# Rows 1024 to 2047 of w_down in pairs by seven products, in both layers of a hybrid attention trunk

## The chip, the cores and the metric

One NeuronCore of one Trainium2 chip runs the whole kernel in one launch. The metric is the time of one execution on the device, in microseconds, median of several runs. The kernel before takes 1486.2 us (1485.95 to 1486.5 in three runs).

## What is computed

Two layers over 512 tokens of width 1024, float32. Each has two attention mixers, and then the part that is at issue here, a squared-ReLU MLP with a residual:

```python
h = rmsnorm(x, norm_mlp)
return x + jnp.square(jax.nn.relu(h @ w_up)) @ w_down
```

w_up is 1024 x 4096, w_down 4096 x 1024. After the second layer comes a last rmsnorm. Products are computed to float32 accuracy from two parts each: every operand is split into a rounded part (hi) and what remains (lo), and TensorE takes hi x hi, hi x lo and lo x hi, three matmuls for one.

## The kernel before, in words

Activations stand transposed, with 128 features on the partitions and the 512 tokens along the free dimension. x is eight tiles of 128 x 512.

**Plain products** are blocks of 128 x 128 weights against 512 columns (`gemm`, L244 to L246, three matmuls a block). Their weights come by SP's DMA queue in pieces of 128 x 1024 (`fetch`, L202), in an order written out by hand (`order`); `convert` makes hi on ScalarE (L218) and lo on VectorE (L219), one piece ahead of the use.

**Seven products** (a Strassen scheme in Winograd's form) take the place of eight for a 2 x 2 block product: 256 of the rows, 256 of the contraction's halves and 256 tokens. `Strassen.unit` computes one of 16 units of w_up, 256 hidden features each: products a11, s1, a12, s2, a22, s3, s4, each of twelve matmuls of 256 columns (`narrow`, L1535). s2 and s3 add onto a11's bank, s4 onto s1's. The sums of the left operand are made from two raw blocks: r2 and r1 are loaded by SP, POOL's queue adds one half of r2 to the other while transferring (L1487), a third block is loaded and added to as well (L1495, L1496), and `convert` of Strassen adds (L1522, L1525) and splits into hi and lo (L1515, L1516). A unit runs the conversion of the next unit between its products. ScalarE and VectorE take the results out of PSUM into z (L1557 to L1577), `act` applies relu, the norm's factor and the square (L1598, L1599), and splits the result into hi and lo (L1600, L1601). The list `acts` gets two entries a unit, so entries 4c to 4c+3 are the rows 512c to 512c+511 of w_down.

**w_down**: rows 0 to 3071 go plainly, in six chunks of four blocks of rows. For each chunk and each of the eight column blocks m, one plain result of twelve 512-column matmuls (`down` in `mlp`) is added to x[m] by VectorE (L1124). `DOWNS` says how many of these 48 results follow each unit; three are left over for after unit 15:

```python
DOWNS = 0, 0, 3, 4, 3, 4, 4, 4, 4, 4, 4, 3, 3, 2, 2, 1
```

Rows 3072 to 4095 go by seven products: `combine`, called for units 12 to 15, forms the sums of the right operand from z (L1292 to L1299), and `Strassen.down` (S.down in the text) computes four pairs of column blocks behind it (L1323) and adds them to x (L1342 to L1364). Its first products are a11 and a12 of two tiles, then s2 and so on; a11 takes the even act entries, a12 the odd ones, s2 the sums. It is followed by the next layer, or by the output.

`load(g)` is issued two units ahead. Every engine's queue runs in order, SP's and POOL's included; the order within a queue is set at build time and need not be the order of the code. Tiles are shared by tags with a number of buffers each (`BUFS`), and a new use waits for the last reader of the old.

Of the kernel before, what the change touches and what calls it, by code (L numbers as in the profile page):

```python
# [18 lines left out]
D = 1024  # L19
T = 512  # L20
# [65 lines left out]
def layout(a):  # L86
# [3 lines left out]
    for l in range(L):  # L90
# [53 lines left out]
class Body:  # L144
# [8 lines left out]
    BUFS = dict(raw=2, wh=2, wl=2, u2=8, o2=8, va=4, t2=12, kd=2, kk=1, zz=4, zzm=2, pt=10, long=2, q2=3, q2m=1, vn=1, e=2, cp=2, a4=4, b4=4, f=2, h=2, tmp=3,  # L153
# [42 lines left out]
    def fetch(self):  # L196

        if self.plan and self.plan[0] is not None:
            src, n, *tag = self.plan.popleft()
            tag = tag[0] if tag else self.raws.popleft() if self.raws else "raw"  # L200
            raw = self.t(tag, [128, 1024], name="raw")
            self.nc.sync.dma_start(raw[:, :n], src)  # L202
            self.loaded.append((raw, src, n))
# [419 lines left out]
    def compress(self, kc, vc, small, l):  # L623
# [3 lines left out]
        for x, pos in ((kc, "pos_k"), (vc, "pos_v")):  # L627
            t = [self.t("t2", [128, 8, 2, 32], name="ca") for _ in range(2)]
            v = x.rearrange("p (n j r) -> p r j n", j=8, r=2)
            for half in range(2):  # L630
                nc.vector.memset(t[half][:, :, 1, 31], 0.0)
# [138 lines left out]
    def setup(self, first):  # L770
# [15 lines left out]
        self.kcz = t[:, 512:1280].rearrange("p (h f n) -> p h f n", h=2, f=2)  # L786
        self.vz = t[:, 1408:1920].rearrange("p (h r d) -> p h r d", h=2, r=2)
# [50 lines left out]
    def order(self, l):  # L838
# [23 lines left out]
        yield from ((a["wd2"][l, c, m], 1024) for c in range(6) for m in range(4))  # L862

    def layer(self, l, u):
# [227 lines left out]
        for m in range(8):  # L1092
# [20 lines left out]
    DOWNS = 0, 0, 3, 4, 3, 4, 4, 4, 4, 4, 4, 3, 3, 2, 2, 1  # L1113

    def mlp(self, l, x, S, acc):
# [4 lines left out]
        def down(c, m, w):  # L1120

            ps = self.p(self.short())
            yield from self.gemm(ps, w, 4 * (m % 2), acts[4 * c:4 * c + 4], ks=4)
            nc.vector.tensor_add(x[m], x[m], ps)  # L1124

        def downs():
            for c in range(6):
# [56 lines left out]
    def go(self):  # L1184
# [20 lines left out]
        self.xs = [self.dp.tile([128, T], F32, name=f"xs{k}") for k in range(KT)]  # L1205
        self.x_src = [a["xT"][k] for k in range(KT)]
# [10 lines left out]
class Strassen:  # L1217
# [9 lines left out]
    def __init__(self, body, l, x, gm):  # L1227
        self.b, self.nc, self.l, self.x, self.gm = body, body.nc, l, x, gm
        self.raw, self.ops = {}, {}
        self.c, self.t, self.twice, self.made, self.done = [], [], [], 0, set()  # L1230
# [56 lines left out]

    AHEAD = 8

    def combine(self, p):  # L1290

        b, V = self.b, self.nc.vector  # L1292
        v = self.c[p].rearrange("p a c -> p (a c)").rearrange("p (k c) -> p k c", c=256)
# [6 lines left out]
        self.t.append(o)  # L1300

    def down(self, acts):
# [9 lines left out]
        def side(k):  # L1312
            if k not in known:
                i = dict(s1=0, s2=3, s3=1, a22=2)[k]
                known[k] = [(t[:, i, 0], t[:, i, 1]) for t in self.t]
            return known[k]

        def product(k, g, onto=None):
# [6 lines left out]
            if self.twice:  # L1325
                xs, self.twice = xs[:2] + self.twice, []
# [129 lines left out]
    def source(self, g, i):  # L1456
        a = self.b.a
        return (a["wup"][self.l, 2 * g + i] if g < 16 else a["wdn"][self.l, 2 * g + i - 32]).rearrange("p k c -> p (k c)")

    def load(self, g, third=True):  # L1460

        b = self.b
        if g > 17:
            r = b.t("vn", [128, 2, 1024], name="raw") if g == 18 else b.t("kk", [128, 4, 1024], name="raw")[:, :2]
# [3 lines left out]
        else:  # L1468
# [5 lines left out]
            if g < 2:  # L1474
                for t in (r2, r1, s3):
# [167 lines left out]
```

## Time and profile before

| | |
|---|---|
| median of three runs | 1486.2 us |
| profiled execution, first to last instruction | 1485.2 us |
| TensorE matmuls busy | 1477.2 us |
| TensorE weight loads busy | 1290.5 us |
| VectorE busy | 1137.4 us |
| ScalarE busy | 804.7 us |
| GpSimd (POOL) busy | 109.1 us |
| moved by DMA | 203.65 MB |
| granted TensorE clock | 0.997 of 2.4 GHz |

The profiled execution's total time outside its span is not given; the span is 1.0 us below the median of the runs. Busy matmul time is modelled at the ends and overlaps, so distances between starts tell more than durations. PEld is TensorE's weight load, which runs beside the matmuls; DVE is VectorE, ACT ScalarE, SP and POOL the other two engines with DMA queues. In layer 0 the MLP's units run from 412.6 to 688 us, S.down from 699.5 to about 740 us.

### The profile page before, as it was taken

Reading aid. Unit: us, or ns where it says so; the run is one execution under the profiler, and the core shown is the slowest. Engines: PE = TensorE matmul, PEld = TensorE weight load, DVE = VectorE, ACT = ScalarE, POOL = GpSimd, SP = SyncE. Lnnn points to the kernel's source line nnn. Section 1 sums busy time; section 2 is a strip of 40 time slices with the busy share of each in tenths; the row PEclk is TensorE's granted clock in tenths of the full one; section 3 lists DMA queues with packets and bytes.
Section 4 is the critical chain, followed back from the end, with each engine's and each line's share of the span. In section 5 each row is a group of like instructions: output and inputs, shape, how many; then the busy total and the mean of one; then the engine's idle time right before and its main releaser. Section 6 shows DMA issues by size and latency. Waiting matters only on the chain.

```text
span 1485.2 us, 23423 instructions
## 1 busy us (share of the span) xinstructions
PE 1477.2 (99%) x8766; PEld 1290.5 (87%) x8766; DVE 1137.4 (77%) x2247; ACT 804.7 (54%) x1533; POOL 109.1 (7%) x159
## 2 busy tenths in 40 slices
PE   9999999999999999999999999999999999999998
PEld 8887888888899988999988788888888999999998
DVE  5688988777986767779746789787679977667885
ACT  6465655554774444456444656555447644444554
POOL 1010000001000000002010000000010100000121
PEclk9999999999999999999999999999999999999998
DMA  7554522126554555456256543221274645545561
GB/s 272 168 152 128 165 71 72 57 72 206 176 138 127 156 154 142 143 149 184 79 197 181 167 118 114 80 77 58 97 216 128 176 142 148 146 123 147 156 143 57
DMA packets 75649, 203.65 MB, mean 137 GB/s; under 512 B 9456, under 2 KB 10864, under 8 KB 75536
## 3 DMA queue, kind: packets, MB, share of 16 engines
q1 hardware_dynamic: 58832, 172.24, 35.9%
q0 software_dynamic: 12672, 23.07, 9.3%
q10 hardware_dynamic: 4032, 6.84, 1.3%
q8 instruction: 69, 1.13, 0.3%
q14 instruction: 44, 0.36, 0.1%
HBM read 151.72 MB, written 4.19 MB: 105 GB/s over the span
## 4 chain that ended last, share of the span: by engine, by line
PE 95%; DVE 2%; issue 1%; ACT 0%; DMA 0%; POOL 0%; POOLq 0%; SPq 0%; DVEq 0%; ACTq 0%
PE ps_mm L244 12%; PE ps_mm L245 12%; PE ps_mm L246 12%; PE ps_S L1535 9%; PE ps_PT L1535 6%; PE ps_O L244 3%; PE ps_O L245 3%; PE ps_O L246 3%; PE ps_mm L1535 3%; PE ps_O L1535 3%; PE ps_O L614 3%; PE ps_PT L587 2%; PE ps_S L562 2%; PE ps_mm L1323 2%; PE ps_S L1323 2%; PE ps_PT L472 1%
## 5 line engine op out<-in xcount | busy, mean ns | idle before, releaser
L218 ACT CAST wh<-raw 128x1024 fp32r<-128x1024 f32 (+2 forms) x161 | 164.5, 1023 | 147.3 <-PE ps_O L245 81.1
L219 DVE TENSOR_TENSOR wl<-raw,wh 128x1024 fp32r<-128x1024 f32 (+2 forms) x161 | 191.8, 1192 | 17.8 <-ACT wh L218 14.8
L244 PE MATMUL ps_mm<-u,wh 128*128 128x512 f32 x480 | 192.4, 401 | 0.2
L245 PE MATMUL ps_mm<-u,wh 128*128 128x512 f32 x480 | 189.3, 394 | 0.0
L246 PE MATMUL ps_mm<-u,wl 128*128 128x512 f32 x480 | 188.9, 393 | 0.0
L1516 DVE TENSOR_TENSOR s<-raw,s 128x1024 fp32r<-128x1024 f32 (+1 forms) x128 | 138.9, 1087 | 32.5 <-ACT s L1515 31.3
L244 PE MATMUL ps_mm<-o,wh 128*128 128x512 f32 x344 | 134.6, 391 | 0.0
L245 PE MATMUL ps_mm<-o,wh 128*128 128x512 f32 x344 | 134.5, 391 | 0.0
L246 PE MATMUL ps_mm<-o,wl 128*128 128x512 f32 x344 | 134.2, 390 | 0.0
L1515 ACT CAST s<-raw 128x1024 fp32r<-128x1024 f32 (+1 forms) x128 | 118.0, 942 | 20.7 <-PE ps_PT L1535 9.1
L244 PEld LDWEIGHTS ps_mm<-u,wh 128*128 128x128 f32 x480 | 90.3, 188 | 20.0 <-issue 1.5
L246 PEld LDWEIGHTS ps_mm<-u,wl 128*128 128x128 f32 x480 | 90.2, 188 | 19.2
L245 PEld LDWEIGHTS ps_mm<-u,wh 128*128 128x128 f32 x480 | 90.4, 188 | 15.3 <-issue 0.4
L1535 PE MATMUL ps_S<-t,s 128*128 128x256 f32 x768 | 98.1, 277 | 0.1
L1535 PEld LDWEIGHTS ps_S<-t,s 128*128 128x128 f32 x768 | 92.1, 188 | 0.4 <-ACT z L1565 0.3
L550 ACT ACTIVATE E<-E,tiny 128x384 f32<-128x384 f32 (+3 forms) x112 | 65.5, 585 | 48.4 <-DVE tiny L549 48.2
L244 PE MATMUL ps_O<-o,wh 128*128 128x512 f32 x224 | 87.2, 389 | 0.0
L245 PE MATMUL ps_O<-o,wh 128*128 128x512 f32 x224 | 87.2, 389 | 0.0
L246 PE MATMUL ps_O<-o,wl 128*128 128x512 f32 x224 | 87.2, 389 | 0.0
L549 DVE CUSTOM_DVE_ANT_0 E<-ps_S,ct 128x384 f32<-128x384 f32 (+3 forms) x112 | 56.9, 515 | 31.6 <-PE ps_S L562 31.3
L246 PEld LDWEIGHTS ps_mm<-o,wl 128*128 128x128 f32 x344 | 64.6, 188 | 13.6
L245 PEld LDWEIGHTS ps_mm<-o,wh 128*128 128x128 f32 x344 | 64.6, 188 | 12.6 <-DVE o L504 0.3
(362 smaller groups left out, 3305.6 us busy)
## 6 DMA issues: line engine op xcount, KB each, us to landing
raw<-wb SPq DMA_DIRECT2D x64, 512.0 KB, 3.3
raw<-wup SPq DMA_DIRECT2D x64, 512.0 KB, 4.5
raw<-wd SPq DMA_DIRECT2D x48, 512.0 KB, 3.6
raw<-raw POOLq DMA_DIRECT2D x88, 256.0 KB, 4.1
w<-w SPq DMA_DIRECT2D x32, 256.0 KB, 5.3
kda<-hla SPq DMA_DIRECT2D x32, 256.0 KB, 3.7
q2a<-hla SPq DMA_DIRECT2D x64, 128.0 KB, 2.3
raw<-wo SPq DMA_DIRECT2D x16, 512.0 KB, 4.2
```

What stands on the lines that cost most here:

```text
L218: nc.scalar.copy(h[:, :n], raw[:, :n])
L219: nc.vector.tensor_tensor(lo[:, :n], raw[:, :n], h[:, :n].bitcast(F32), op=OP.subtract)
L244: mm(ps, h[:, c], xh, start=start and i == 0, stop=False)
L245: mm(ps, h[:, c], xl, start=False, stop=False)
L246: mm(ps, lo[:, c], xh, start=False, stop=stop and i == ks - 1)
L549: nc.vector.tensor_tensor_reduce(e, ps, self.mask[:, T - n:], -1.0, BIG, OP.add, OP.min, mx)
L550: nc.scalar.activation(e, e, AF.Exp, bias=mx, scale=-1.0, accum_out=un["sm"][:, i:i + 1])
L614: nc.tensor.matmul(O[:, bank, :, q:], v, pt[g][f][:, :, c:c + 256 - q], start=br == 0 and b == 0 and f == 0, stop=False)
L1323: mm = lambda o, *z, **kw: nc.tensor.matmul(o, *z, skip_group_check=True, **kw)
L1515: nc.scalar.copy(h, src)
L1516: nc.vector.tensor_tensor(lo, src, h.bitcast(F32), op=OP.subtract)
L1535: mm = lambda o, *z, **kw: self.nc.tensor.matmul(o, *z, skip_group_check=True, **kw)
```

## The change

Rows 1024 to 2047 (act entries 8 to 15, from units 4 to 7) no longer go plainly but in four pairs by seven products, steps 20 to 23, placed between unit 8 and unit 9. The plain chunks are now four: rows 0 to 1023 ahead of the pairs, 2048 to 3071 behind. While the first 16 plain results are made x is in HBM (`xm`): w_out's loop writes it there from ACT's queue, ScalarE copies each plain result to a staging tile, and POOL's queue adds two of them at a time to HBM. A pair makes its two column blocks of w_down's sum in an SBUF tile y, and one accumulating transfer each adds x from HBM to it (`SUMS`, at steps 22, 23, 9 and 10). From then on the y tiles are x.

`KEPT` names the units whose z is kept and combined, now eight. `act` treats both halves of z in one instruction, after s4. A load for a pair does without the third block's addition by DMA, and VectorE does it (`g > 19`). No weight is fetched ahead across the pairs (`yield None`, `behind`).

```diff
-        yield from ((a["wd2"][l, c, m], 1024) for c in range(6) for m in range(4))
+        yield from ((a["wd2"][l, c, m], 1024) for c in range(2) for m in range(4))
+        yield None
+        yield from ((a["wd2"][l, c, m], 1024) for c in (2, 3) for m in range(4))
...
             acc = self.sumsq(x[m], acc, True)
+            nc.scalar.dma_start(self.xm[m // 2][:, m % 2], x[m])
...
-    DOWNS = 0, 0, 3, 4, 3, 4, 4, 4, 4, 4, 4, 3, 3, 2, 2, 1
+    STEPS = list(range(9)) + [20, 21, 22, 23] + list(range(9, 16))
+    DOWNS = 0, 0, 3, 4, 3, 3, 2, 1, 0, 0, 0, 0, 0, 0, 4, 4, 4, 3, 1, 0
+
+    SUMS = {22: 0, 23: 1, 9: 2, 10: 3}
...
-            yield from self.gemm(ps, w, 4 * (m % 2), acts[4 * c:4 * c + 4], ks=4)
-            nc.vector.tensor_add(x[m], x[m], ps)
+            yield from self.gemm(ps, w, 4 * (m % 2), acts[(0, 4, 16, 20)[c]:][:4], ks=4)
+            if c > 1:
+                nc.vector.tensor_add(x[m], x[m], ps)
+                return
+            if m % 2 == 0:
+                self.stage = self.t("st", [128, 2, T], name="y")
+            nc.scalar.copy(self.stage[:, m % 2], ps)
+            if m % 2:
+                nc.gpsimd.dma_start(self.xm[m // 2], self.stage, accum_op=OP.add)
...
-        for g, n in enumerate(self.DOWNS):
-            for h in {14: (16, 17), 15: ()}.get(g, (g + 2,)):
-                S.load(h)
+        steps = self.STEPS + [16, 17]
+        S.follow = dict(zip(steps, steps[1:]))
+        for i, (g, n) in enumerate(zip(self.STEPS, self.DOWNS)):
+            if g < 14 or 19 < g:
+                S.load(steps[i + 2])
+            elif g == 14:
+                S.load(16)
+                S.load(17)
+            if g in self.SUMS:
+                p = self.SUMS[g]
+                nc.gpsimd.dma_start(S.y[p], self.xm[p], accum_op=OP.add)
+            if g > 19:
+                S.pair(g, D, n, acts[8:16])
+                if g == 23:
+                    x[:] = [y[:, i] for y in S.y for i in range(2)]
+                    self.fetch(S.y[3][:, 0])
+                continue
             S.unit(g, D, n, acts, acc)
-            if g > 11:
-                S.combine(g - 12)
+            if g in S.KEPT:
+                S.combine(g)
+            if g == 9:
+                self.ahead()
...
+    KEPT = 4, 5, 6, 7, 12, 13, 14, 15
...
+        if g < 8:
+            o = [b.t("ta", [128, 1024], F32R, name="ta").rearrange("p (a k c) -> p a k c", a=2, c=256)
+                 for _ in range(2)]
+            for i, t in enumerate(o):
+                w = v[:, 2 * i:2 * i + 2]
+                self.nc.scalar.copy(t[:, :, 0], w)
+                V.tensor_tensor(t[:, :, 1], w, t[:, :, 0].bitcast(F32), op=OP.subtract)
+            self.t.append([t[:, i] for t in o for i in range(2)])
+            return
...
+    def pair(self, g, D, n, acts):
+
+        b, nc = self.b, self.nc
+        V, A = nc.vector, nc.scalar
+        conv = self.convert(self.follow[g])
+        lo, hi = slice(0, 256), slice(256, 512)
+        half = lambda i, s: [(h[:, s], r[:, s]) for h, r in acts[i::2]]
+        sums = lambda i: [(t[i][:, 0], t[i][:, 1]) for t in self.t]
+        side = dict(a11=(half, 0, lo), a12=(half, 1, lo), s4=(half, 1, hi),
+                    s1=(sums, 0), s2=(sums, 3), s3=(sums, 1), a22=(sums, 2))
+        y = b.t("xb", [128, 2, T], name="x")
+        self.y.append(y)
+
+        def product(i, onto=None):
+            ps = b.bank()[:, :256] if onto is None else onto
+            f, *z = side[i]
+            self.narrow(ps, g, i, onto is None, f(*z))
+            return ps
+
+        m = product("a11")
+        A.copy(y[:, 1, lo], m)
+        next(conv, None)
+        p5 = product("s1")
+        A.activation(y[:, 0, hi], p5, AF.Copy, scale=-1.0)
+        next(conv, None)
+        ps = product("a12")
+        V.tensor_tensor(y[:, 1, lo], y[:, 1, lo], ps, op=OP.add)
+        product("s2", m)
+        A.copy(y[:, 1, hi], m)
+        next(conv, None)
+        ps = product("a22")
+        A.activation(y[:, 0, lo], ps, AF.Copy, scale=-1.0)
+        product("s3", m)
+        v = y[:, 0].rearrange("p (k c) -> p k c", k=2)
+        V.tensor_tensor(v, v, m[:, None, :].to_broadcast([128, 2, 256]), op=OP.subtract)
+        next(conv, None)
+        product("s4", p5)
+        V.tensor_tensor(y[:, 1, hi], y[:, 1, hi], p5, op=OP.add)
+        for _ in range(n):
+            next(conv, None)
+            next(D)()
+        run(conv)
...
-        self.nc.gpsimd.dma_start(s3, self.raw[g][0][:, :512], accum_op=OP.add)
+        if g < 20:
+            self.nc.gpsimd.dma_start(s3, self.raw[g][0][:, :512], accum_op=OP.add)
...
         split(r1, "a11", "a12")
         yield
+        if g > 19:
+            nc.vector.tensor_tensor(s3, a11, s3, op=OP.add)
         nc.vector.tensor_tensor(a11, s1, a11, op=OP.add)
...
-        self.act(z[:, 0], acts, tag)
         next(conv, None)
         product("s4", p5)
         V.tensor_tensor(z[:, 1, hi], z[:, 1, hi], p5, op=OP.subtract)
-        if g > 11:
-            self.c.append(z)
-        self.act(z[:, 1], acts, tag)
+        if g in self.KEPT:
+            self.c[g] = z
+        self.act(z, acts, tag)
...
+        V.scalar_tensor_tensor(c, c, 0.0, self.R[:, None, :].to_broadcast([128, 2, T]), op0=OP.max, op1=OP.mult)
+        A.activation(c, c, AF.Square)
...
-        if tag == "a4" and len(acts) in (29, 31):
-            t = b.t("t2", [128, 2, 256], F32R, name="twice")
-            nc.scalar.copy(t, self.late[:, :2])
-            self.twice.append((t[:, 0], t[:, 1]))
+        for (h, lo), w in parts:
+            A.copy(h, w)
+            V.tensor_tensor(lo, w, h.bitcast(F32), op=OP.subtract)
```

Besides, the weights are laid out anew on the host, buffers are added and renumbered (`ta`, `a2`, `a3`, `ca`, `st`, `xb`, 8 to 32 KB a partition each), and a column of zeros in the attention's `compress` is copied from a constant instead of being set.

## Rows read from the trace of the kernel before

**Rows 1.** The page's first part: busy us (share of the span) xinstructions

```profile
PE 1477.2 (99%) x8766; PEld 1290.5 (87%) x8766; DVE 1137.4 (77%) x2247; ACT 804.7 (54%) x1533; POOL 109.1 (7%) x159
```

**Rows 2.** The chain that ended last, in time order: start us, us, what

```profile
429.65 1.41 PE ps_O L1535 x12
...
530.93 1.42 PE ps_S L1535 x12
532.35 1.38 PE ps_PT L1535 x12
533.73 1.36 PE ps_mm L1535 x12
...
539.17 1.36 PE ps_PT L1535 x12
...
699.56 1.42 PE ps_PT L1323 x12
```

**Rows 3.** Timeline of TensorE, 520 to 560 us: start us, us, instruction

```profile
519.87 0.39 PE L244 MATMUL ps_mm<-o,wh 128*128 128x512 f32 x1
...
530.54 0.39 PE L246 MATMUL ps_O<-o,wl 128*128 128x512 f32 x1
530.77 1.58 PE L1535 MATMUL ps_S<-b,s 128*128 128x256 f32 x12
```

**Rows 4.** Busy time by stretch; columns: length, engines' busy us, clock, DMA share, GB/s

```profile
core 0: us, PE busy (x) PEld busy (x) DVE busy (x) ACT busy (x) POOL busy (x), PEclk, DMA share, GB/s
423.16:433.89 10.73, 10.73 (x95) 10.73 (x94) 8.80 (x18) 7.62 (x15) 1.74 (x2) 1.00 0.76 212
530.93:551.42 20.49, 20.49 (x134) 18.61 (x134) 14.48 (x19) 9.57 (x15) 1.75 (x2) 1.00 0.49 142
678.56:699.50 20.94, 20.82 (x133) 18.71 (x133) 19.53 (x31) 14.46 (x25) 5.21 (x6) 1.00 0.95 239
699.50:742.00 42.50, 42.50 (x352) 41.68 (x351) 31.89 (x62) 18.94 (x33) 1.75 (x2) 1.00 0.21 65
```

**Rows 5.** Instructions by line and shape: xcount | busy us, mean ns | idle before

```profile
L219 DVE TENSOR_TENSOR wl<-raw,wh 128x1024 fp32r<-128x1024 f32 x151 | 184.4, 1222 | 14.0 <-ACT wh L218 13.3 <-issue 0.2
...
L1598 DVE SCALAR_TENSOR_TENSOR z<-z,tiny 128x512 f32<-128x512 f32 x64 | 43.6, 684 | 0.0
...
L1124 DVE TENSOR_TENSOR x<-x,ps_mm 128x512 f32<-128x512 f32 x48 | 32.8, 684 | 3.9 <-PE ps_mm L246 3.6
...
L1522 DVE TENSOR_TENSOR raw<-raw 128x512 f32<-128x512 f32 x32 | 22.0, 686 | 0.0
...
L591 ACT CAST pth<-ps_PT 128x512 fp32r<-128x512 f32 x32 | 18.6, 580 | 31.3 <-PE ps_PT L587 31.3
...
L1563 DVE TENSOR_TENSOR z<-ps_mm,z 128x256 f32<-128x256 f32 x26 | 11.0, 423 | 39.1 <-PE ps_mm L1535 36.5 <-ACT d L1264 1.4 <-ACT s L1515 1.1
```

**Rows 6.** Timeline of all engines, 676 to 704 us, end of layer 0's units

```profile
685.27 0.62 PE L1535 MATMUL ps_PT<-b,s 128*128 128x256 f32 x4
...
686.01 1.68 PE L1535 MATMUL ps_S<-t,s 128*128 128x256 f32 x12
...
687.53 1.10 PE L1535 MATMUL ps_PT<-b,s 128*128 128x256 f32 x8
...
690.31 0.41 DVE L1577 TENSOR_TENSOR z<-z,ps_PT 128x256 f32<-128x256 f32 x1
...
691.85 0.42 DVE L1601 TENSOR_TENSOR ohl<-z,ohl 128x256 fp32r<-128x256 f32 x1
...
697.66 1.23 DVE L1299 TENSOR_TENSOR tt<-z,tt 128x1024 fp32r<-128x1024 f32 x1
```

**Rows 7.** The page's DMA queues: packets, MB, share; then one issue by ACT

```profile
q1 hardware_dynamic: 58832, 172.24, 35.9%
q0 software_dynamic: 12672, 23.07, 9.3%
...
715.24 0.33 ACTq L1380 DMA_DIRECT2D xs<-x  x1
```

More of the change, by code (lines that the diff above doesn't have):

```diff
@@ L192, with fetch @@
     bank_o, held = 0, None
-    def fetch(self):
+    def fetch(self, behind=None):
+        if behind is not None:
+            assert self.plan.popleft() is None
         if self.plan and self.plan[0] is not None:
@@ L201, in fetch @@
             raw = self.t(tag, [128, 1024], name="raw")
+            if behind is not None:
+                self.nc.gpsimd.tensor_copy(raw[:, :1], behind[:, :1])
             self.nc.sync.dma_start(raw[:, :n], src)
@@ L627, in compress @@
         for x, pos in ((kc, "pos_k"), (vc, "pos_v")):
-            t = [self.t("t2", [128, 8, 2, 32], name="ca") for _ in range(2)]
+            t = self.t("ca", [128, 2, 8, 2, 32], name="ca")
+            t = [t[:, 0], t[:, 1]]
             v = x.rearrange("p (n j r) -> p r j n", j=8, r=2)
             for half in range(2):
-                nc.vector.memset(t[half][:, :, 1, 31], 0.0)
+                nc.vector.tensor_copy(t[half][:, :, 1, 31], self.zeros)
                 o = OFF[pos] + 8 * half
@@ L1205, in go @@
         self.xs = [self.dp.tile([128, T], F32, name=f"xs{k}") for k in range(KT)]
+        self.xm = [self.dp.tile([128, 2, T], F32, name=f"xm{k}") for k in range(KT // 2)]
         self.x_src = [a["xT"][k] for k in range(KT)]
@@ L1229, in __init__ @@
         self.raw, self.ops = {}, {}
-        self.c, self.t, self.twice, self.made, self.done = [], [], [], 0, set()
+        self.c, self.t, self.y, self.made, self.done = {}, [], [], 0, set()
     PARTS = [("a11", 0), ("a12", 0), ("a11", 1), ("a12", 1), ("s2", 0), ("s2", 1), ("s3", 0), ("s3", 1),
@@ L1299, in combine @@
         V.tensor_tensor(o[:, :, 1], v, o[:, :, 0].bitcast(F32), op=OP.subtract)
-        self.t.append(o)
+        self.t.append([o[:, i] for i in range(4)])
+    def pair(self, g, D, n, acts):
[37 more added lines that the diff above has]
+        run(conv)
     def down(self, acts):
@@ L1314, in side @@
                 i = dict(s1=0, s2=3, s3=1, a22=2)[k]
-                known[k] = [(t[:, i, 0], t[:, i, 1]) for t in self.t]
+                known[k] = [(t[i][:, 0], t[i][:, 1]) for t in self.t]
             return known[k]
@@ L1457, in source, with load @@
         a = self.b.a
-        return (a["wup"][self.l, 2 * g + i] if g < 16 else a["wdn"][self.l, 2 * g + i - 32]).rearrange("p k c -> p (k c)")
-    def load(self, g, third=True):
+        if g < 16:
+            return a["wup"][self.l, 2 * g + i].rearrange("p k c -> p (k c)")
+        return a["wdn"][self.l, int(g < 20), 2 * (g % 4) + i].rearrange("p k c -> p (k c)")
+    def load(self, g, third=True, mark=None):
         b = self.b
-        if g > 17:
-            r = b.t("vn", [128, 2, 1024], name="raw") if g == 18 else b.t("kk", [128, 4, 1024], name="raw")[:, :2]
+        if 17 < g < 20:
+            r = b.t("vn", [128, 2, 1024], name="raw") if g == 18 else b.t("kk", [128, 2, 1024], name="raw")[:, :2]
             if g == 18:
@@ L1474, in load @@
             if g < 2:
+                mark = b.mark
+            if mark is not None:
                 for t in (r2, r1, s3):
-                    self.nc.gpsimd.tensor_copy(t[:, :1], b.mark)
+                    self.nc.gpsimd.tensor_copy(t[:, :1], mark)
         r1, r2, s3 = self.raw[g] = r1[:, :1024], r2[:, :1024], s3[:, :512]
-        if g > 17:
+        if 17 < g < 20:
             self.nc.sync.dma_start(r2, self.source(g, 0))
@@ L1530, in convert, with narrow @@
         yield
-    def narrow(self, ps, g, i, new):
+    def narrow(self, ps, g, i, new, xs=None):
         h, lo = self.ops[g].pop(i)
+        xs = xs or [(x[:, 0], x[:, 1]) for x in self.xs[i]]
         mm = lambda o, *z, **kw: self.nc.tensor.matmul(o, *z, skip_group_check=True, **kw)
@@ L1537, in narrow @@
             c = slice(p * 128, (p + 1) * 128)
-            x = self.xs[i][p]
-            mm(ps, h[:, c], x[:, 0], start=new and p == 0, stop=False)
-            mm(ps, h[:, c], x[:, 1], start=False, stop=False)
-            mm(ps, lo[:, c], x[:, 0], start=False, stop=p == 3)
+            xh, xl = xs[p]
+            mm(ps, h[:, c], xh, start=new and p == 0, stop=False)
+            mm(ps, h[:, c], xl, start=False, stop=False)
+            mm(ps, lo[:, c], xh, start=False, stop=p == 3)
     def unit(self, g, D, n, acts, acc):
@@ L1545, in unit @@
         V, A = nc.vector, nc.scalar
-        conv = self.convert(g + 1)
+        conv = self.convert(self.follow[g])
         def product(i, onto=None):
```

49 lines of the change are left out of this document (27 added, 22 removed).

## Prediction

> **What bounds the kernel now.** I read the page's first part, then the chain that ended last, then single stretches of the MLP. TensorE is busy 99% of the span; VectorE, next, 77% [rows 1]. A busy matmul row says little by itself, so look at starts. In a plain stretch 48 matmuls of 512 columns start from 519.87 to 530.77 us, 0.227 us apart [rows 3]. Behind them the seven products of a w_up unit follow each other on the chain: 1.42, 1.38, then 1.36 us for twelve matmuls of 256 columns [rows 2], 0.113 us each, exactly half. The whole step with four plain results takes 20.49 us [rows 4]: 7 x 1.36 + 0.08 = 9.6, and 4 x 12 x 0.227 = 10.9. There is no gap in it. So the MLP is limited by the number of columns TensorE streams, and a change is worth what it takes from that, less what the other engines then fail to hide. They hide well where plain results stretch a step: VectorE has 14.48 us of work in those 20.49 [rows 4].
>
> **The change: columns.** Per layer 16 plain results go (two chunks by eight column blocks): 16 x 12 x 0.227 = 43.6 us. Four pairs by seven products come: 28 x 1.36 = 38.1 us. That is 5.5 us less. The 0.08 us at each return from 512 to 256 columns (1.42 + 1.38 against 2 x 1.36) is paid after 14 steps now, after 11 then (counted in DOWNS): 0.2 us less. Both layers: **11.5 us less**. That the price halves with the columns is what the rows say. The Trainium skill (TensorE: Matmul & The Clock Gate, Back-to-back issue gap) speaks against it: it gives a sustained 81 ns a matmul at 128 columns and 131 ns at 512, which read along a line is an estimate of 98 ns at 256; then the pairs would cost 32.8 us, the plain results 25.2, and the change would lose 15 us over both layers. Rows 2 and 3 show 113 and 227 ns instead, and I go by them.
>
> **VectorE.** A step with four plain results has 14.48 us of it [rows 4], of which the plain results are 4 x 0.684 (adds into x) and 2 x 1.222 (halves of weights), 5.2 [rows 5]. A unit alone is thus 9.3 us against TensorE's 9.5. A pair step drops act (two multiplications and two subtractions, 4 x 0.684 = 2.7) and its conversion has one more 512-column addition (0.686): 7.2 us. A kept unit adds a combine: 0.686 + 2 x 0.423 + 2 x 0.686 = 2.9 us. So VectorE falls behind by 0.5 us in unit 7 (one plain result: 9.3 + 2.9 + 0.6 against 12.3) and 0.5 in unit 8, regains 2.3 in each pair, and falls behind 1.0 in unit 9, where the next weight is also converted. Converted weights wait most of a step before they are used, and unit 1 already runs without plain results: its 10.73 us are seven products and the normalisation's matmuls, with VectorE at 8.80 [rows 4]. Bounds for this stretch: 0 to 2 us a layer; I take 0.5, near the row of unit 1.
>
> **ScalarE.** The first 16 plain results leave PSUM through ScalarE now, at 0.58 us by the nearest copy [rows 5], 9.3 us a layer spread over six steps in which it has half its time free (9.57 of 20.49) [rows 4]; if that cover went, a result's bank would come free late, three results on. In unit 1 it works 7.62 of 10.73 us. Act now treats both halves after the last product: evacuation 0.4, multiplication 1.4 (2 x 0.684), square and copy 1.2 each (2 x 0.58), 4.2 us; were the next unit's first copy queued behind that, it would end at 4.5, and TensorE wants it with its fourth product, 3 x 1.36 = 4.1 us on. So 0.4 us at each of four places where a unit without plain results follows: 0 to 1.6 us a layer; I take 0, since the trace shows ScalarE's and TensorE's instructions placed out of program order when an operand is late: four matmuls of s4 start before s3, eight after [rows 6].
>
> **Pace.** After an interruption products run at 1.41 instead of 1.36 [rows 2], with the weight loads filling the whole stretch (10.73 of 10.73) [rows 4]. All 42 products of the six steps at that pace: 2.1 us a layer; none: 0. I take 0.3, since beside plain results the pace is 1.36 throughout. The Trainium skill (Trainium Kernel Development and Optimization, Performance Expectations) has the share of weight loads rather than of matmuls as the measure of headroom; by it a stretch of 256 columns has none (100% against 18.61 of 20.49), which would put this term at its upper bound.
>
> **The end of the MLP.** Now unit 15 is followed by four plain results, 10.9 us; then by none (DOWNS ends 3, 1, 0). Behind unit 15's last product VectorE's work runs from about 688.4 us (eight matmuls after 687.53) to 698.9: evacuation, act, combine [rows 6]; S.down starts at 699.56 [rows 2]. VectorE is 19.53 of 20.94 us busy there [rows 4]. Of the 10.5 us three adds go (2.1): 8.4 remain. What is late next: a11 and a12 of the first two tiles need only act, and their first three row blocks not even unit 15; they fill 5.4 us, and three row blocks of s2 twice 2.0 more. Units 14 and 15 also bring VectorE behind by 1.1 and 2.5 us (9.3 + 2.9 + 1.3 against 12.3; 12.0 against 9.5), after steps with slack. Bounds: 0 to 8.4 us a layer. I take 0.8: 8.4 less 7.4, with the lag held by S.down's slack, where VectorE has 31.89 of 42.50 us.
>
> **Transfers.** SP's and ACT's queue moves 172.24 MB in 35.9% of the span, 323 GB/s; POOL's accumulating one 23.07 MB in 9.3%, 167 GB/s [rows 7]. A unit's loads, 1.31 MB and two accumulations of 256 KB, need 4.1 + 3.1 = 7.2 us of all engines (0.76 of unit 1, the row says). Pairs spare one accumulation. A sum of 512 KB costs 3.1 us more, a weight 1.6: steps 22, 23 and 9 need 10.3, 11.9 and 11.9 us in steps of 9.5, 5.6 too many in all. Loads have a step in hand, and unit 10 lasts 20 us; so 0 to 5.6 us a layer, and I take 0, by the row of unit 1, which fits. The eight accumulations of plain results fall in steps of 12 to 20 us, where the share is 0.49. POOL's queue is in order: a sum waits for a pair's y, and the additions for later loads stand behind it, which is the same 5.6. The eight writes of x to HBM take 0.33 us of issue each on ACT's queue [rows 7], 2.6 us during w_out, right behind an instruction that waits for the same x: nothing, at most 2.6. The moved weight load behind y on SP holds only the load for unit 11, which has a whole step. The constant column copied instead of set, and the two copies that go (L1605), are off the path: nothing either way.
>
> **Sum.** -11.5 + 2 x (0.5 + 0 + 0.3 + 0.8 + 0) = -8.3 us. The profiled execution spans 1485.2 us; it stands 1.0 below the median of the runs, 1486.2, and I keep that 1.0. So 1476.9 by the span and **1477.9** by the median: 1478.0.
>
> **Rivals.** A measurement can tell about 0.2%, 3.0 us: faster means under 1483.2, slower over 1489.2.
> - A, the forecast, 1474.5 (nothing given back) to 1483: 0.70. For it: TensorE has no gap in any step of the MLP, though VectorE was at its limit in units 0 and 1.
> - B, transfers decide in the group: all 5.6 us a layer come back, 1477.9 + 11.2 = 1489.1, or half of it, 1483.5. Then conversions wait for additions in HBM or SBUF, and evacuations queue behind them. For it: a share of 0.95 already in the last step [rows 4]. Against: the loads lead by a step. 0.15, centred on 1486.
> - C, slower: the end of the MLP. Unit 15's act and combine stand bare because the last plain results have moved ahead; TensorE waits the full 8.4 us and the lag of 2.5 in each layer: 1477.9 + 2 x (8.4 - 0.8 + 2.5) = 1498; the chain alone gives 1493. It decides from 6.5 us a layer (1489.2 needs 2 x 5.7 more than the 0.8 taken). For it: S.down starts 0.7 us after that chain ends. Against: the a11 and a12 products don't need combine. 0.12.
> - D, the change doesn't do what it says, since 256 columns don't cost half in these operands (a fixed price a matmul, or 1.42 throughout and more): 28 x 1.56 would cancel the gain, 1486. Nothing in the rows reaches 1.56, and the page's 15 us of loss is this mechanism carried further: 0.03, a third of it slower.
>
> **Numbers.** Faster 0.72 (A, and the light end of B), same 0.13, slower 0.15 (C, the heavy end of B, D's third). The range leaves out C and the heaviest of B: 1474.0 to 1488.0; A alone is 1474.5 to 1483.
>
> **What would show it.** Right: in the chain of waits 28 more products a layer of 1.36 to 1.41 us on a new line between unit 8 and unit 9, 192 fewer plain matmuls, unit 8 to unit 10 in 57 to 59 us, S.down's first product within 2 us of unit 15's last. B shows as VectorE or ScalarE idle behind DMA raw or x in steps 23 to 10; C as TensorE idle over 5 us ahead of S.down. A gap elsewhere (w_out, attention, whose buffers have moved) would make the prediction wrong.

## The result: 21 us slower, where 8 us less were forecast

The changed kernel takes 1507.3 us (median of four runs, 1505.6 to 1513.3) against 1486.2 for the kernel before: a ratio of 1.0149, 95% interval 1.013 to 1.0168. The forecast was 1478.0, range 1474 to 1488. The profiled execution took 1506.54 us, with a span of 1504.8.

### The profile page after: what moved, and what is told of

It reads as the page before. It is cut to its first block, busy times and chain, and to the rows that moved or that the text cites. A ratio compares the mean times of both kernels' runs of the same rounds, so it can differ in the third digit from the quotient of the medians.

```text
span 1504.8 us, 24178 instructions
## 1 busy us (share of the span) xinstructions
PE 1480.3 (98%) x9054; PEld 1305.4 (87%) x9054; DVE 1155.8 (77%) x2239; ACT 837.4 (56%) x1577; POOL 137.8 (9%) x193
## 4 chain that ended last, share of the span: by engine, by line
PE 88%; DMA 4%; DVE 4%; issue 2%; ACT 1%; POOL 0%; SPq 0%; POOLq 0%; DVEq 0%; ACTq 0%
PE ps_mm L249 11%; PE ps_mm L250 11%; PE ps_mm L251 11%; PE ps_S L1635 8%; PE ps_PT L1635 6%; PE ps_mm L1635 4%; PE ps_O L1635 3%; PE ps_O L619 2%; PE ps_PT L592 2%; PE ps_O L251 2%; PE ps_O L249 2%; PE ps_O L250 2%; DMA raw<-raw 2%; PE ps_S L567 2%; PE ps_mm L1417 2%
## 5 line engine op out<-in xcount | busy, mean ns | idle before, releaser
L1613 DVE TENSOR_TENSOR s<-raw,s 128x1024 fp32r<-128x1024 f32 (+1 forms) x160 | 173.3, 1086 | 37.7 <-ACT s L1612 37.3
L223 ACT CAST wh<-raw 128x1024 fp32r<-128x1024 f32 (+2 forms) x145 | 147.4, 1020 | 81.3 <-PE ps_mm L250 24.0
L249 PE MATMUL ps_mm<-u,wh 128*128 128x512 f32 x480 | 192.3, 401 | 0.2
L250 PE MATMUL ps_mm<-u,wh 128*128 128x512 f32 x480 | 189.1, 394 | 0.0
L224 DVE TENSOR_TENSOR wl<-raw,wh 128x1024 fp32r<-128x1024 f32 (+2 forms) x145 | 171.8, 1186 | 14.2 <-ACT wh L223 11.5
L1612 ACT CAST s<-raw 128x1024 fp32r<-128x1024 f32 (+1 forms) x160 | 147.7, 941 | 37.5 <-PE ps_PT L1635 9.1
L250 PE MATMUL ps_mm<-o,wh 128*128 128x512 f32 x280 | 110.2, 394 | 7.0 <-DVE o L1708 7.0
L249 PE MATMUL ps_mm<-o,wh 128*128 128x512 f32 x280 | 110.0, 393 | 1.5 <-ACT o L1707 1.5
L251 PE MATMUL ps_mm<-o,wl 128*128 128x512 f32 x280 | 109.7, 392 | 0.0
L249 PEld LDWEIGHTS ps_mm<-u,wh 128*128 128x128 f32 x480 | 90.3, 188 | 20.0 <-issue 1.5
L250 PEld LDWEIGHTS ps_mm<-u,wh 128*128 128x128 f32 x480 | 90.3, 188 | 15.3 <-issue 0.4
L596 ACT CAST pth<-ps_PT 128x384 fp32r<-128x384 f32 (+1 forms) x96 | 47.4, 510 | 49.6 <-PE ps_PT L592 49.6
L1593 POOL DMA_DIRECT2D raw<-raw x40 | 36.7, 916 | 357.0 <-DMA raw<-wup 244.5
L250 PEld LDWEIGHTS ps_mm<-o,wh 128*128 128x128 f32 x280 | 52.7, 188 | 17.8 <-DVE o L1708 7.4
L597 DVE TENSOR_TENSOR ptl<-ps_PT,pth 128x384 fp32r<-128x384 f32 (+1 forms) x96 | 55.9, 598 | 14.0 <-ACT pth L596 13.3
L1690 ACT ACTIVATE z<-z 128x1024 f32<-128x1024 f32 x32 | 34.0, 1061 | 56.9 <-DVE z L1689 56.5
```

Source lines behind the costliest of these rows:

```text
L223: nc.scalar.copy(h[:, :n], raw[:, :n])
L224: nc.vector.tensor_tensor(lo[:, :n], raw[:, :n], h[:, :n].bitcast(F32), op=OP.subtract)
L249: mm(ps, h[:, c], xh, start=start and i == 0, stop=False)
L250: mm(ps, h[:, c], xl, start=False, stop=False)
L251: mm(ps, lo[:, c], xh, start=False, stop=stop and i == ks - 1)
L596: nc.scalar.copy(h[:, e, :n], ps[:, :n])
```

## The profile after

The page's first part and its two large queues, to be held against [rows 1] and [rows 7]:

```profile
PE 1480.3 (98%) x9054; PEld 1305.4 (87%) x9054; DVE 1155.8 (77%) x2239; ACT 837.4 (56%) x1577; POOL 137.8 (9%) x193
...
q1 hardware_dynamic: 59984, 174.34, 36.8%
q0 software_dynamic: 17280, 37.76, 14.5%
```

The change was made as described: 288 more matmuls, which is 672 narrow ones more and 384 plain ones less, and 14.7 MB more through the accumulating queue. But TensorE's busy time rose by 3.1 us and its idle time by 16.5 us (8.0 to 24.5). The view of waits, TensorE alone (instruction, what it waited for, us in total, times, longest), says where:

```profile
PE ps_mm L250 <- DVE o L1708: 7.0, 2, 4.0
PE ps_mm L1417 <- ACT ohl L1707: 3.7, 1, 3.7
PE ps_S L1417 <- DVE z L1671: 2.5, 1, 2.5
PE ps_mm L249 <- ACT o L1707: 1.5, 2, 1.0
PE ps_O L1635 <- DVE x L1390: 1.3, 1, 1.3
```

The longest in the kernel before, by the same view, lies outside the MLPs and is there in both kernels:

```profile
PE ps_PT L1202 <- DVE ones L1199: 1.1, 1, 1.1
```

All five above are new, and all lie in the two MLPs: 16.0 us. L249 and L250 are the first plain results behind the group; L1417 is S.down; L1390 is the last addition of a pair (pair 23 of layer 1). So, but for the last row, there are **two places**, one behind the group of pairs and one at the end of the units, each in both layers.

To see what the stretches cost I take the starts of the first matmul of every step. The two right columns are runs of the next section. All in us:

| stretch | before | after | sums late | sums late, tail late |
|---|---|---|---|---|
| start of unit 0, layer 0 | 412.5 | 413.8 | 413.2 | 412.9 |
| unit 0 to S.down, layer 0 | 286.9 | 291.1 | 284.5 | 284.7 |
| of that, units 10 and 11 (41.0 with eight plain results and no wait) | 38.3 (seven results) | 48.8 | 42.2 | 42.3 |
| S.down, layer 0 | 40.6 | 44.6 | 46.5 | 39.8 |
| from there to unit 1 of layer 1 | 417.6 | 419.2 | 419.5 | 420.2 |
| unit 1 to S.down, layer 1 | 276.1 | 279.6 | 274.3 | 274.7 |
| of that, units 10 and 11 | 38.3 (seven results) | 46.7 | 42.9 | 43.2 |
| S.down, layer 1 | 40.6 | 45.9 | 48.2 | 42.2 |

The 40.6 of layer 0 before contain 1.4 us of the next layer, whose first six wide matmuls run ahead of S.down's last product there; in the other columns they run behind it.

**Behind the group.** Busy time by stretch, with the columns of [rows 4]; the four stretches are pairs 21 and 22, pair 23, unit 9, and the first half of unit 10:

```profile
558.00:576.00 18.00, 18.00 (x155) 18.00 (x155) 13.59 (x17) 8.23 (x14) 4.26 (x5) 1.00 0.99 241
576.00:586.00 10.00, 10.00 (x87) 10.00 (x86) 6.73 (x9) 5.91 (x9) 2.60 (x3) 1.00 0.97 242
586.00:595.40 9.40, 9.40 (x85) 9.40 (x84) 6.95 (x9) 5.22 (x9) 1.95 (x3) 1.00 1.00 286
595.40:605.00 9.60, 8.53 (x66) 7.69 (x64) 5.05 (x7) 4.57 (x6) 0.86 (x1) 1.00 0.98 306
```

The share of the DMA engines is 0.97 to 1.00 for 47 us on end; the plain step of [rows 4] has 0.49. VectorE is not the limit here: it is busy 5.05 of 9.60 us just where TensorE begins to wait. Its timeline, and that of POOL, at that moment:

```profile
599.23 1.22 DVE L1689 SCALAR_TENSOR_TENSOR z<-z,tiny 128x1024 f32<-128x1024 f32 x1
605.19 0.69 DVE L1621 TENSOR_TENSOR raw<-raw 128x512 f32<-128x512 f32 x1 [4.75 <-DMA raw<-wup]
605.92 0.69 DVE L1624 TENSOR_TENSOR raw<-raw 128x512 f32<-128x512 f32 x1
606.53 1.22 DVE L1613 TENSOR_TENSOR s<-raw,s 128x1024 fp32r<-128x1024 f32 x1
607.66 1.22 DVE L1708 TENSOR_TENSOR o<-z,o 128x1024 fp32r<-128x1024 f32 x1
```
```profile
587.17 0.89 POOL L1164 DMA_DIRECT2D x<-xm  x1 [0.80 <-POOL raw L206]
589.77 0.87 POOL L1583 DMA_DIRECT2D raw<-raw  x1 [1.71 <-DMA raw<-wup]
597.05 0.86 POOL L1593 DMA_DIRECT2D raw<-raw  x1 [6.40 <-issue]
```

TensorE's two waits beside them:

```profile
603.53 0.50 PE L249 MATMUL ps_mm<-o,wh 128*128 128x512 f32 x1 [1.04 <-ACT o L1707]
...
608.93 0.79 PE L250 MATMUL ps_mm<-o,wh 128*128 128x512 f32 x1 [3.96 <-DVE o L1708]
```

Read it backwards. TensorE wants unit 9's act, the lo part of which VectorE makes (L1708). The hi part is there by 603.53, when the wait on L1707 ends, so L1708 could run then. But ahead of it in VectorE's queue stands an addition for unit 11's weights (L1621) that waits for transfers. The row names a load (raw<-wup), but what landed last is the accumulation that reads the tile L1621 overwrites, issued at 597.05 and landed at 605.0. It is issued so late because the load that it reads was late. The timeline puts the 6.40 us ahead of it down to `issue`, that is, to nothing, but POOL's queue stood in that accumulation's semaphore wait (count, then ns three times, then its start in us):

```profile
L1593 POOLq EVENT_SEMAPHORE  x1: 6687/6687/6687, 589.8 to 589.8; - x1
```

The wait ends at 596.45, and the semaphore of unit 11's second load, issued at 587.24, counts up in the trace from 594.70 to 596.42. So 512 KB took 9.2 us to land, where the median of such loads is 4.5. Ahead of it in SP's queue stand two of the four w_down loads (586.39), and beside it runs the last sum of x (587.17).

The Trainium skill (DMA: Bandwidth & Descriptors, Issuing engines are not separate DMA queues) has transfers from any engine run interleaved on the same 16 DMA engines. The packets of the trace agree: from 592 to 598 us those of the accumulating queue hold 0.61 of the engines' time and those of the load queue 0.44, one full set together.

**At the end of the units.** Timeline of TensorE where S.down begins, then two rows of VectorE ahead of it:

```profile
704.84 1.18 PE L1417 MATMUL ps_PT<-ohl,d 128*128 128x256 f32 x9
705.86 1.18 PE L1417 MATMUL ps_O<-ohl,d 128*128 128x256 f32 x9
706.88 1.18 PE L1417 MATMUL ps_mm<-ohl,d 128*128 128x256 f32 x9
707.90 1.18 PE L1417 MATMUL ps_S<-ohl,d 128*128 128x256 f32 x9
708.92 0.39 PE L1417 MATMUL ps_mm<-ohl,d 128*128 128x256 f32 x2
712.97 0.58 PE L1417 MATMUL ps_mm<-ohl,d 128*128 128x256 f32 x1 [3.66 <-ACT ohl L1707]
```
```profile
703.75 0.69 DVE L1299 TENSOR_TENSOR raw<-raw 128x512 f32<-128x512 f32 x1 [2.65 <-DMA raw<-raw]
...
708.97 0.41 DVE L1676 TENSOR_TENSOR z<-z,ps_PT 128x256 f32<-128x256 f32 x1
```

TensorE does what the prediction said it could: nine matmuls, three row blocks, of each of a11 and a12 in two tiles. That is 4.1 us (704.84 to 708.92), and then it stands until unit 15's act is there. That act was never close: unit 15's last evacuation (L1676) comes at 708.97, four us behind unit 15's last product, since VectorE had waited for a transfer and then worked off operands of S.down and splits of the combine's sums.

**What a wait costs on top.** After both waits the granted clock is down, and it is at the lower of its two levels (1.2 of 2.4 GHz) right behind the second:

```profile
605.00:614.90 9.90, 5.96 (x30) 5.78 (x31) 5.12 (x6) 2.75 (x6) 1.76 (x2) 0.66 0.67 179
712.90:716.00 3.10, 3.03 (x14) 3.04 (x15) 2.96 (x8) 1.55 (x5) 1.44 (x2) 0.50 1.01 176
```

In layer 1 it is 0.72 from 1353 to 1356 us and 0.55 from 1453 to 1456, behind waits of 3.0 and 2.5 that end at 1353.2 and 1452.0. A product on the chain takes 2.56 us there (610.15) instead of 1.36. So a wait costs more than its length: units 10 and 11 lose 7.8 us in layer 0, of which the waits are 5.0, and some 1.3 stay in experiments 1 and 2, where the waits there are 0.9 or less.

## Experiments

The edits of runs 1 and 2 are shown against the changed kernel, that of run 3 against run 2, and all others against run 3; "..." stands for lines left out.

**1. The four sums of x left out.**

```diff
-                nc.gpsimd.dma_start(S.y[p], self.xm[p], accum_op=OP.add)
+                pass
```

> Leaves out the four transfers per layer that add the residual and the first 16 plain results from HBM onto the pairs' y (the SUMS table); the output misses x and those results. Theory T (transfers): the 16 DMA engines are full from unit 22 to unit 10 because these sums (3.1 us each by the queue's mean, 10 us under load) meet the units' loads and the burst of four w_down loads; the first plain results behind the group wait for unit 9's act, which stands on VectorE behind an accumulated load. Without the sums units 10 and 11 of layer 0 take 41 us together instead of 48.8, of layer 1 again 41 instead of 46.7 and the 1.5 us in pair 23 go: 13 to 15 us less, 1492 to 1494, with the wait of S.down (3.9 and 5.3 us) still there. Rival W (the burst of w_down loads alone is enough, or VectorE is late on its own): the wait at units 10 and 11 stays above 4 us a layer and the time falls by less than 6 us.

1497.3 us (ratio to before 1.0075, 1.006 to 1.009): 10.0 less than the changed kernel. Units 10 and 11 together fall from 48.8 (layer 0) and 46.7 us (layer 1) to 42.2 in both. The wait in pair 23 is gone, and the wait at S.down is longer (4.3 us in layer 0). Less than expected by 3 us, since about 1.3 us a layer of the excess in units 10 and 11 stays, unit 9 of layer 0 is 1.0 us longer (10.54) and S.down of layer 0 2.2.

**2. The same sums, two to four steps later.**

```diff
-    SUMS = {22: 0, 23: 1, 9: 2, 10: 3}
+    SUMS = {11: (0, 1), 12: (2, 3)}
...
-                nc.gpsimd.dma_start(S.y[p], self.xm[p], accum_op=OP.add)
+                for p in self.SUMS[g]:
+                    nc.gpsimd.dma_start(S.y[p], self.xm[p], accum_op=OP.add)
```

> The same four sums, but issued with units 11 (pairs 20 and 21) and 12 (pairs 22 and 23), in steps of 20 and 18 us where the DMA share was 0.4 to 0.5; all is computed. Theory T: as without the sums, 13 to 15 us less, 1492 to 1494, the share of the DMA engines in the group under 0.9 and units 11 and 12 without a wait. Rival W: less than 6 us. A third outcome: the wait moves, since POOL's queue is in order and a sum issued in unit 12 holds back the additions for later loads; then unit 13 or 14 is over its length of 12.3 and 10 us by some us.

1496.7 us (1.007, 1.0053 to 1.0086): 10.6 less than the changed kernel, with everything computed; again short of the 13 to 15 expected, since S.down takes some 2 us a layer more than in the changed kernel (table above). It matters where the sums stand, not that they are there: the run without them is no faster. Busy time by stretch, the same first and third stretch as above:

```profile
558.00:576.00 18.00, 18.00 (x155) 18.00 (x154) 13.96 (x19) 9.65 (x15) 2.61 (x3) 1.00 0.71 188
...
586.00:595.40 9.40, 9.40 (x85) 9.40 (x84) 7.73 (x10) 6.14 (x10) 1.73 (x2) 1.00 0.99 317
```

The pairs have transfers to spare again; only unit 9's stretch, with its four w_down loads, is still full. The third outcome (later units held up by POOL's queue) did not come: units 12 and 13 take 20.49 and 17.77 us, as without a wait. The waits of TensorE that are left stand at S.down:

```profile
PE ps_mm L1417 <- ACT ohl L1707: 4.3, 1, 4.3
PE ps_S L1417 <- DVE z L1671: 3.9, 1, 3.9
PE ps_mm L249 <- ACT o L1707: 1.1, 2, 0.9
```

**3. Late sums, and two plain results behind unit 15.**

```diff
-    DOWNS = 0, 0, 3, 4, 3, 3, 2, 1, 0, 0, 0, 0, 0, 0, 4, 4, 4, 3, 1, 0
+    DOWNS = 0, 0, 3, 4, 3, 3, 2, 1, 0, 0, 0, 0, 0, 0, 4, 4, 4, 2, 0, 0
```

> As the late sums, and the last two plain results of each layer stand behind unit 15 again (the table ends 4, 4, 4, 2, 0, 0 instead of 4, 4, 4, 3, 1, 0); all is computed. Theory C (the end of the MLP is bare): two results of 2.7 us give 5.4 us of cover for unit 15's act, so S.down's first nine row blocks wait no longer: S.down takes 41 us instead of 44.6 and 45.9, 6 to 9 us less than the late sums alone. Rival E: VectorE is late there because it waits for accumulated loads (2.65 us in front of unit 15's combine), so the wait only moves: less than 3 us.

1487.9 us (1.0012, 1.0002 to 1.0021; ten runs from 1485.8 to 1489.9): 8.8 less again, at the upper end of what was expected. S.down falls to 39.8 and 42.2 us. The same view of waits:

```profile
PE ps_mm L249 <- ACT o L1707: 1.6, 2, 1.3
...
PE ps_mm L1417 <- ACT ohl L1707: 0.4, 1, 0.4
```

So two results of 2.7 us were enough. The moved cover was the cause at this end, and not the accumulated loads alone.

**4. And unit 15's act in two halves again.**

```diff
+        if g == 15:
+            self.half(z, 0)
         next(conv, None)
         product("s4", p5)
...
+        if len(acts) == 30:
+            self.half(c, 1)
```

> As the run with late sums and late tail, and unit 15's act is again in two halves, the first ahead of product s4 as before the change; all is computed. If the merged act is part of what is late, S.down's first wait shortens by up to 1.5 us a layer against the run before it, 1 to 3 us in all; if the tail already covers it, the times are within 1 us of each other.

1488.05 us (1.0015, 1.0005 to 1.0024), the same as without it. The merged act costs nothing that can be seen once the tail is covered.

**5 to 7. The pace of the pairs.** Every pair takes 9.92 us, where 7 x 1.36 = 9.52 were counted, in all runs so far (but for the one pair with a wait). The chain of waits of run 3, pair 20, product by product:

```profile
545.54 1.42 PE ps_mm L1635 x12
546.96 1.44 PE ps_S L1635 x12
548.40 1.38 PE ps_PT L1635 x12
549.78 1.42 PE ps_mm L1635 x12
```

a11 and the four products on sums take 1.42 to 1.44, a12 and s4 1.38. The latter read the tile `oo`, whose content begins 48 floats behind the start of its tile; the others read `oe` and `ta`, which begin at theirs. From the addresses in the built program, `ta` and the weights begin at the same offset modulo 512 bytes, `oo` 192 bytes off. Three runs test this: `ta` shifted by 48 floats in two packings, and the shift of `oo` taken away. The first two also change the padding of other tiles; run 5 drops a staging buffer, and run 6 spreads the last plain results as 4, 4, 2, 2, 2, 0.

```diff
-            o = [b.t("ta", [128, 1024], F32R, name="ta").rearrange("p (a k c) -> p a k c", a=2, c=256)
+            o = [b.t("ta", [128, 1072], F32R, name="ta")[:, 48:].rearrange("p (a k c) -> p a k c", a=2, c=256)
```
```diff
-                even, odd = (o[:, 0], o[:, 1]), (lambda t: (t[:, 48:560], t[:, 560:1072]))(b.t("a3", [128, 1152], F32R, name="oo"))
+                even, odd = (o[:, 0], o[:, 1]), (lambda t: (t[:, :512], t[:, 512:1024]))(b.t("a3", [128, 1152], F32R, name="oo"))
```

> As the run with late sums and late tail; the tiles ta (the sums of unit 4 to 7) begin 48 floats (192 bytes) later and the padding of oo, ohl and the second stage buffer go, so that in 230 instead of 672 of the 3360 narrow matmuls the moving operand and the weights begin at the same offset modulo 512 bytes; all is computed. Theory P: a matmul of 256 columns takes 120 ns where those offsets are equal and 113 where they differ, so a pair takes 9.6 us instead of 9.92, and the whole 2 to 3 us less than the run with late tail. Rival S: the slower pace is a state that follows an interruption and stays until wide matmuls come, whatever the addresses; then the products on ta stay at 120 ns and the pairs at 9.9 us.

> The same shift of ta in another packing (243 equal offsets of 3360, both stage buffers kept), and the last plain results spread as 4, 4, 2, 2, 2, 0 with two behind unit 15; all is computed. Theory P: pairs of 9.6 us again, and about the time of the run before it, 1484 to 1487; rival S: pairs of 9.9 us.

> The opposite: as the run with late sums and late tail, but the 48 floats in front of oo are taken away, so that the a12 and s4 products of the pairs, too, have equal offsets (864 of 3360); all is computed. Theory P: matmuls on oo go from 113 or 114 ns to 120, a pair from 9.92 to 10.08 us. Rival S: they stay at 113 or 114, the pair at 9.92.

The third came out to the digit: pairs of 10.06 to 10.08 us, all seven products at one pace (a row of the chain there, a product on `oo`):

```profile
548.97 1.44 PE ps_PT L1635 x12
```

It took 1487.9 us in its one run. The first two missed: 1499.4 us (1.0084, 1.007 to 1.0098) and 1494.2 (1.0052, 1.0039 to 1.0064), with pairs of 9.9 and 9.8 us. Tiles whose size is no multiple of 512 bytes put all others at odd offsets. Over these runs, run 3 and run 9, narrow matmuls start 120 ns apart (median) where the two offsets are equal modulo 256 bytes, 118 where they are 128 apart and 114 to 117 elsewhere; with everything scattered the shift won little. And plain matmuls in those packings went from 227 to 231 ns and more: in run 5 a step with four plain results takes 20.94 us instead of 20.49. Summed over all distances between starts, run 5 has 5.4 us more than run 3 in the wide matmuls and 4.6 in the narrow ones of the units, 10.0 of its 11.5. A packing that shifts `ta` and leaves all other offsets was not run, so what it would give stays open.

**9. The opposite for wide matmuls.**

```diff
-            h = self.t("wh", [128, 1024], F32R)
-            lo = self.t("wl", [128, 1024], F32R)
+            h = self.t("wh", [128, 1152], F32R)[:, 48:1072]
+            lo = self.t("wl", [128, 1152], F32R)[:, 48:1072]
```

> As the run with late sums and late tail, but the converted weights wh and wl of the wide matmuls (512 columns) begin 48 floats later in tiles of 1152, so that 40 instead of some 920 of each 1024 have equal offsets modulo 512 bytes; all is computed. Theory P2 (read from the two runs with shifted tiles): wide matmuls run at 227 ns where the offsets are equal and at 232 where they are not, the other way round than the narrow ones; some 2700 matmuls by 5 ns are 13 us more, 1499 to 1503. Rival: the two runs were slower because of their packing (buffers, waits) and not of the pace; then the time stays within 3 us of the run with late tail.

1496.6 us (1.007, 1.0056 to 1.0083): 8.8 more than run 3, less than the 13 expected. The starts of wide matmuls in w_out's stage of layer 0 go from 227.4 to 233.1 ns in the mean; in the MLP of layer 0 only from 227.7 to 229.5. So the 13 us were too many because not all wide matmuls lose the whole 5 ns: summed over all their distances they cost 4.0 us. Another 2.0 of the 8.8 are a wait that run 3 doesn't have, in unit 10 of layer 1 for unit 9's act; the rest isn't placed. The direction held.

**8, 10, 11. What is left behind the group.** In run 3 units 10 and 11 still take 1.3 (layer 0) and 2.3 us (layer 1) more than 41.0. Run 8 holds back two of the four w_down loads until unit 9's act is done; run 10 begins the plain results with unit 11, run 11 with two in unit 10 (its table ends 2, 4, 4, 3, 1, 0). The first diff is run 8's, the second run 10's.

```diff
+            if behind is None and self.hold:
+                behind = self.hold.popleft()
...
+                self.hold = deque([None, acts[-1][0].bitcast(F32)])
```
```diff
-    DOWNS = 0, 0, 3, 4, 3, 3, 2, 1, 0, 0, 0, 0, 0, 0, 4, 4, 4, 2, 0, 0
+    DOWNS = 0, 0, 3, 4, 3, 3, 2, 1, 0, 0, 0, 0, 0, 0, 0, 4, 4, 4, 2, 0
-    SUMS = {11: (0, 1), 12: (2, 3)}
+    SUMS = {12: (0, 1), 13: (2, 3)}
```

> As the run with late sums and late tail, and of the four w_down loads that are issued in a burst when pair 23 is done, the third waits on POOL for unit 9's act (SP's queue is in order, so the fourth stands behind it); all is computed. Theory W' (what is left of the wait in unit 10, 12.96 us and 13.89 where 11.7 is free of waits, comes from the burst that fills the transfers from 586 to 596 us and makes unit 9's act late): unit 10 and 11 take 41.0 to 41.5 us together instead of 42.3 and 43.2, and the whole is 1 to 3 us less than the run with late tail, 1485 to 1487. Rival L: unit 9's act is late by its own chain (conversion, multiplication, square, copy: 5 us behind unit 9's last product); then units 10 and 11 stay over 42 us.

> As the run with late sums and late tail, but the plain results behind the group begin with unit 11 instead of unit 10 (the table ends 0, 4, 4, 4, 2, 0 and two results stand behind unit 15), and the sums are issued with units 12 and 13; all is computed. Theory L (the first plain results need unit 9's act at once, whose chain on VectorE and ScalarE ends 5 us behind unit 9's last product): with a unit in between nothing waits, units 9 to 15 with 14 plain results and two more take 7 x 9.6 + 16 x 2.73 = 110.9 us a layer instead of 112.5 and 113.5; 2 to 4 us less in all, 1483.5 to 1486. Rival: another operand is late there (the loads of units 11 and 12 from the full stretch, 586 to 596 us), and the wait moves to unit 10 or 11; then the time stays within 1.5 us.

> Between the two: two plain results in unit 10 (the table ends 2, 4, 4, 3, 1, 0 and two behind unit 15), the sums with units 12 and 13; all is computed. Theory L: the first of them still needs unit 9's act, so most of the wait in unit 10 stays (0.5 to 2 us a layer), 1485 to 1488. Rival: if the loads are what is late, the same as with the plain results one unit later.

Run 8: 1486.5 us (1.0004, 0.9995 to 1.0013), units 10 and 11 unchanged at 42.3 and 43.1, though the share of the DMA engines from 586 to 596 us falls from 0.98 to 0.76: the burst is not it, as rival L had it. (Unit 9 of layer 0 is 1.2 us longer there; the test is clean in layer 1 alone.) Run 10: 1487.2 (1.0007, 0.9998 to 1.0016), no gain either. The wait for act is gone there, as theory L said, and another came in its place:

```profile
PE ps_PT L1635 <- DVE s L1613: 1.5, 2, 0.8
```

Unit 10 now waits some 0.8 us in each layer for a converted weight, and units 11 and 12 take 42.2 us where 41.0 would do. Run 11: 1487.4 (1.0011, 1.0003 to 1.002), in between, with unit 9's act still late (1.6 us at most). I read this as VectorE being a little behind here whatever comes next, so that the order of the plain results only chooses who waits; no run gave it less to do. None of these versions beats the kernel before: runs 8 and 10 are level with it within what can be measured, runs 3 and 11 about 0.1% above.

## Why the prediction was wrong, by its own steps

- **Columns, -11.5**: right in size for what went, short for what came. Plain steps keep their lengths (20.49, 17.77), so 43.6 us a layer did go; the 28 products took 4 x 9.92 = 39.7 instead of 38.1. The step "pace ... I take 0.3" had the bounds right (0 to 2.1) and the value wrong: 1.6. The argument "beside plain results the pace is 1.36 throughout" was read from products on operands that lie 192 bytes off the weights' offset, and says nothing of tiles that don't. The 0.08 us "at each return" is of this kind too: in the built program of before, six of the twelve matmuls of a unit's first product lie at equal offsets, and unit 2, which has no plain results ahead of it, shows the same 119 ns a matmul in that product.
- **Transfers, "I take 0, by the row of unit 1, which fits"**: this step failed. A surplus was counted (5.6 us a layer, with one w_down load each in steps 23 and 9; the trace has four within 2.2 us) and then forgiven, because "Loads have a step in hand". But a surplus over several steps with no slack between them eats that step: the share stands at 0.97 to 1.00 over 47 us, and a load of unit 11 lands 9.2 us after its issue. Moving the sums gave back 10.6 us, 5.3 a layer, nearly the upper bound. Rival B had this mechanism and the right sign of it in the trace ("VectorE or ScalarE idle behind DMA raw or x").
- **The end of the MLP, "I take 0.8"**: this step failed too. 8.4 us were bare and 7.4 were to be filled by work that doesn't need unit 15. Only 4.1 us of that ran ahead of the wait in layer 0: the four products' first three row blocks had been counted as whole products (5.4), s2's (2.0) never ran there, and the lag of VectorE, put at 2.5 and left to S.down's slack, stood in front of unit 15's act. The tail's return gave 8.8 us, 4.4 a layer. Rival C was this, at some 10 us a layer and so too dear.
- **The rivals excluded one another**: B and C were priced as alternatives with 0.15 and 0.12. As I read the traces they share a cause, little slack on VectorE and on the transfers once the wide matmuls are gone from a stretch, and they came together. The case of both, 1477.9 + 11.2 + 20.2 = 1509 by the prediction's own prices, was not named. 1507.3 was measured, but that the two are so close is in part luck: B gave 10.6 and C 8.8, 12.0 less than their prices, and run 3, without both, still stands 10 us above the forecast for other reasons.
- **VectorE, "I take 0.5"**: the waits for act in units 10 and 11 are its lag; with late sums and late tail these units lose 1.3 and 2.3 us. The row of unit 1 showed no wait since no plain result there needs the act of the unit just before. This dependence, first plain results on unit 9's act, was not in the prediction.
- **ScalarE, "I take 0"**: of the waits on unit 15's merged act 0.4 us are left in run 3, and undoing the merge there (run 4) changes nothing in the time; at the other places it wasn't tested. The rows given for this term show TensorE's matmuls out of program order and say nothing of ScalarE.
- **What run 3 still lacks.** The span of its profiled execution, 1485.3, is that of before, so all 11.5 us of the columns are given back even there: pairs 3.2, units 10 and 11 3.6, between the layers 2.6, S.down of layer 1 1.6 and of layer 0 -0.9, before unit 0 0.5, and about 1 in units 0, 1 and 15. In S.down of layer 1 the products run at 1.41 us from 1444 to 1465 where before they run at 1.36. The chains of waits, run 3 and then the kernel before:

```profile
1443.96 1.41 PE ps_S L1417 x12
```
```profile
1443.55 1.36 PE ps_S L1323 x12
```

  What sets that pace is open: it changes within S.down at the same operands, in the kernel before too. Of the 2.6 us between the layers 1.4 are only a matter of order: in the kernel before six wide matmuls of the next layer run ahead of S.down's last product (737.40 to 738.81 us), in run 3 they run behind it. So 1.2 are lost there, and S.down of layer 0 is 0.5 us longer and not 0.9 shorter. What loses the 1.2 was not tested.
- **Writes of x, 0 to 2.6**: unit 0 begins 0.5 to 1.3 us later in the runs; no run tells whether the writes do that.

## What to carry to other kernels

Count transfers over a whole stretch, not by step: a surplus that no step of the stretch can absorb is paid (here 5.3 of 5.6 us a layer), and it shows as a compute engine that waits in order behind an addition for something it doesn't need yet. When wide work is taken out of a place, ask whose latency it covered there, and put back the least that covers it; here two of 32 results a layer were worth 8.8 us. And if two rivals draw on the same slack, price them together.

## What the runs showed of the hardware that was not expected

The pace of matmuls depends on where operands lie. Narrow ones (256 columns) start 120 ns apart if moving operand and weights begin at the same offset modulo 256 bytes, 113 to 114 in a packing in which they lie 192 off; taking the shift away turned one into the other at once. That isn't all that sets the pace: in S.down of run 3 matmuls that lie 192 off start 118 ns apart (median), and the cause is open. Wide ones (512 columns) are the other way round, 227 ns at equal offsets, 230 to 233 at unequal ones; but in run 5, with all tiles scattered, those at equal offsets take 230 too. The sums of 512 KB took 8.4 us to land (median of eight), one accumulation of 256 KB 10.1, on full DMA engines; the prediction had counted 3.1 and 1.6 us of engine time by the queue's mean, and that is no time to landing. And a wait of TensorE of 2.5 to 4 us is followed by some us at a lower granted clock (0.66 over 9.9 us behind one of them, 0.50 over 3.1 behind another), which makes it dearer than its length.
